# State-space stage: kernel matrix by way of DRAM, per-quarter factors, products summed by accumulating transfers

## The chip, the core and the metric

The kernel runs on one core of a Trainium2 chip. The core has a matrix engine (PE, with its weight loads shown apart as PEld), a vector engine (DVE), a scalar engine (ACT), a general engine (POOL) and a sync engine (SP) whose only work here is to issue transfers. All of them take their instructions in a fixed order and wait on semaphores. Sixteen DMA engines move the data. The metric is device time in microseconds (us). The kernel before takes 2175.32 us, the median of 3 runs (2173.78 to 2179.61).

## The reference

Two layers of a streaming encoder over 256 frames of 2048 channels, in float32. Layer 0 mixes frames with a diagonal state-space model, layer 1 with latent attention; both end in a gated, convolved MLP. The change touches the state-space mixer alone. Its 2048 channels are 128 groups of 16, and each group drives 64 complex states:

```
dt = exp(log_dt);  A = exp(dt * a)                    # per group and state
b' = (A - 1) / a * b
h[t] = A * h[t-1] + b' u[t]                           # u = rmsnorm(x), 16 channels of a group
y[t] = Re(c h[t]) + d_skip * u[t]
y    = gelu(y);  val, gate = split(y @ w_glu + b_glu) # 2048 -> 4096
out  = val * sigmoid(gate)
```

## The kernel before

**Blocks.** The 256 frames are cut into 32 blocks of 8. Within a block, y follows from u by a Toeplitz matrix whose entries are c A^k b' (the kernel matrix), from block to block by the state. The function `s5` goes through the groups in 16 steps (`sb`, 0 to 15) of eight groups (`NG = 2` times `j` 0 to 3); four steps (`PB`) make a quarter of the channels. The 128 partitions hold the real and the imaginary parts of 64 states.

**A step.** `powers` makes, once a quarter, A^0 to A^8 with and without the factor of b' (tile z). `part_a` loads a step's b and c (tile bc, from sBC), scales b with the norm's gain (g4), gives three of the four blocks of bc their signs on ACT (L437 to L439), and multiplies with the powers on DVE: f1 and f2 (output side, nine powers, L448 and L449), e1 and e2 (input side, L451 and L452), and e1 = e1 + e2 (L453). `part_k` turns u (tile U), multiplies f with the last two powers of e on PE to get one row of the kernel matrix (L411, with the skip term L418), copies it to SBUF (tile K, L472), and spreads it to the Toeplitz form: 64 small matmuls with constant selection matrices (C_SL, L482) into two PSUM banks, and two copies to tile TP (L488). `part_e` transposes e1 on PE (L496) and copies it (tile ET, L497). `part_v` multiplies u with ET (tile vs), `part_r` turns vs and rotates it (L515 to L517) and scans over the blocks on DVE (L523), `part_h` rotates back (L528 on PE, L530 to L537 on DVE, tile H), and `part_c` sums TP u and f H on PE and passes the result through Gelu into yg (L549). `frames` makes the sines for the rotations, for two steps at a time (ACT's Sin, L396 and L397).

**The pipeline.** The loop over n issues, in this order: `part_v` of step n-1, `part_c` of n-2, `part_r` of n-1, `part_k` and `part_e` of n, `part_h` of n-1, at the end of a quarter `part_d` (transpose yg and split it into tiles act, L565), then `lead(n+1)`, which is `powers`, `part_a` and `frames` of the next step, and one unit of the matmul with w_glu. So tile TP of a step is read two passes after K was made.

**The w_glu units.** From the first `part_d` on, each pass carries one unit: a load of 1 MB into one of two buffers (raw, L79), a split into a rounded part on ACT (whi, L73) and a rest on DVE (wlo, L74), and 24 matmuls of 512 columns (L108 to L110). 13 of the 32 units lie in the loop; the others follow in `glu_rest`, and then the rest of the network, which the change leaves alone.

**What sets the order.** A list scheduler in the framework orders each engine's instructions when the program is built, with times of its own; the order that it finds is fixed in the program and differs from the written one. All transfers are issued by SP in one queue, in that order: an issue that waits holds up those behind it. Buffers: bc 2, e1 2, e2 1, f1 and f2 3 each, TP 2, raw 2.

Of the kernel before, what the change touches and what calls it, by code (L numbers as in the profile page):

```python
# [40 lines left out]
C_SG, C_NSG, C_TPI, C_FR, C_RS, C_HP, C_MH, C_SL, C_END = 624, 625, 626, 627, 628, 629, 630, 638, 766  # L41
# [3 lines left out]
def tile_trunk(ctx: ExitStack, tc: tile.TileContext, a: dict):  # L45
# [225 lines left out]
    def s5(f):  # L271
        with tc.tile_pool(name="s5", bufs=2) as q1:
# [9 lines left out]
            gX = T(q1, [P, 512], F32, "yg", 1)  # L282
# [50 lines left out]
            Ks = [T(q1, [P, 2, 240], F32, f"K{i}", 1) for i in range(2)]  # L333
            for K in Ks:
                pool.memset(K[:, :, P:], 0.0)
# [5 lines left out]
            dve.tensor_tensor(dB, dB, gX, op=ALU.mult)  # L341
# [14 lines left out]
            def scale_x(rs, qt):  # L356
                c = slice(P * qt, P * qt + P)
                for s in range(8):
                    act.activation(
                        Xn[qt][:, :, 16 * s : 16 * s + 16],  # L360
                        X[s // 4][:, s % 4, c].rearrange("p (g q) -> p g q", q=16),
                        AF.Copy,
                        scale=rs[:, s : s + 1],
                    )

            def powers(qt):
                ps_ = slice(32 * qt, 32 * qt + 32)
# [18 lines left out]
                return z  # L386
# [40 lines left out]
            def flat2(z):  # L427
                return z.rearrange("p s q -> p (s q)")

            def part_a(sb, z):  # L430
# [3 lines left out]
                g4 = T(q1, [P, NP, 16], F32, "g4")  # L434
                sync.dma_start(g4.rearrange("p n q -> p (n q)"), a["sG"][sb].partition_broadcast(P))
                dve.tensor_tensor(bc4[:, 0:2], bc4[:, 0:2], g4.unsqueeze(1).to_broadcast([P, 2, NP, 16]), op=ALU.mult)
                act.activation(bc4[:, 1], bc4[:, 1], AF.Copy, scale=cst[:, C_SG : C_SG + 1])  # L437
                act.activation(bc4[:, 2], bc4[:, 2], AF.Copy, scale=cst[:, C_NSG : C_NSG + 1])
                act.activation(bc4[:, 3], bc4[:, 3], AF.Copy, scale=-1.0)  # L439

                def zt(c, i0, n, t):
                    return z[:, c, i0 : i0 + n, t, h : h + NP].rearrange("p i n -> p n i").unsqueeze(3).to_broadcast([P, NP, n, 16])

                def bc(k, n):
                    return bc4[:, k].unsqueeze(2).to_broadcast([P, NP, n, 16])

                f1, f2 = T(q1, [P, NP, 9, 16], F32, "f1", 3), T(q1, [P, NP, 9, 16], F32, "f2", 3)
                dve.tensor_tensor(f1, zt(0, 0, 9, 1), bc(2, 9), op=ALU.mult)  # L448
                dve.tensor_tensor(f2, zt(1, 0, 9, 1), bc(3, 9), op=ALU.mult)  # L449
                e1, e2 = T(q1, [P, NP, 8, 16], F32, "e1"), T(q1, [P, NP, 8, 16], F32, "e2", 1)  # L450
                dve.tensor_tensor(e1, zt(0, 1, 8, 0), bc(0, 8), op=ALU.mult)  # L451
                dve.tensor_tensor(e2, zt(1, 1, 8, 0), bc(1, 8), op=ALU.mult)  # L452
                dve.tensor_tensor(e1, e1, e2, op=ALU.add)  # L453
                return e1, (f1, f2)

            def part_k(sb, e1, ff):
# [7 lines left out]
                def e67(g, j):  # L464
                    return flat2(e1[:, 4 * g + j, 6:8, :])
# [6 lines left out]
                act.activation(K[:, :, :P], pkg, AF.Copy)  # L472
                TP = T(q1, [P, 4, NG * P], F32, "TP")
                banks = [accb() for _ in range(2)]
                for j in range(2):
                    for odd in range(2):
                        for b in range(4):
                            r = 16 * (2 * b + odd)
                            for jj in range(2):
                                o = C_SL + (2 * j + odd) * 32  # L480
                                hp = slice(64 * jj, 64 * jj + 64)
                                pe.matmul(  # L482
                                    banks[jj][32 * b : 32 * b + 32, j * 256 : (j + 1) * 256].rearrange("p (g c) -> p g c", g=NG),
                                    cst[hp, o : o + 32], K[hp, :, r : r + P],
                                    start=j == 0 and odd == 0, stop=j == 1 and odd == 1, tile_position=(64 * jj, 32 * b),
                                )
                for jj in range(2):
                    act.activation(TP[:, 2 * jj : 2 * jj + 2, :], banks[jj].rearrange("p (j c) -> p j c", j=2), AF.Copy)  # L488
# [51 lines left out]
            def part_c(sb, yg, ff, U, TP, H):  # L540
                def h(g, j):
# [3 lines left out]
                    (lambda g, j: U[:, g, 32 * j : 32 * j + 32], lambda g, j: TP[:, j, g * P : (g + 1) * P]),  # L545
                    *((h, lambda g, j, z=z: flat2(z[:, 4 * g + j, 0:8, :])) for z in ff),
# [5 lines left out]
                    AF.Gelu_apprx_tanh,  # L552
# [40 lines left out]
            for n in range(nb + 2):  # L593
# [522 lines left out]
def _constants():  # L1116
# [8 lines left out]
    c[:, C_DM : C_DM + 16] = (p[:, None] % 32 - 16) == np.arange(16)[None, :]  # L1125
# [11 lines left out]
    for j in range(4):  # L1137
        for odd in range(2):
            q = np.arange(16)
            c[32 * j + 16 + q, C_SL + (2 * (j % 2) + odd) * 32 + 16 * odd + q] = 1.0  # L1140
# [3 lines left out]
def _arrays(i):  # L1144
# [8 lines left out]
    def blocks(re, im):  # L1153
# [18 lines left out]
        "sG": g("norm_g")[0, 0].reshape(4, 16, 2, 16).transpose(1, 2, 0, 3).reshape(16, P),  # L1172
# [37 lines left out]
```

## Time and profile before

| | us |
|---|---|
| median of 3 runs | 2175.32 (2173.78 to 2179.61) |
| the profiled execution | 2179.64, with a span of 2177.9 |
| PE, DVE, ACT, POOL busy in the span | 2080.4, 1402.3, 1130.8, 18.0 |
| state-space loop, from the first product to the last transposes of `part_d` | about 25 to 257 |
| the 16 scans (L523), first and last start | 48.8, 248.7 |
| 64 selection matmuls of all 16 steps (L482) | 33.7 busy on PE |

The times of a row of a view are those of one profiled execution, counted from the first instruction. "busy" adds the durations of the instructions of an engine; two neighbours may overlap by some hundredths of a microsecond, and matmuls by more. "idle before" is time in which the engine stood still ahead of such an instruction, with what ended it. The chain of waits goes back from the last instruction to what released it each time.

### The profile page before, as it was taken

To read this page: it belongs to the slowest core of one execution; us is meant where nothing else is said; L and a number is where in the kernel's file an instruction comes from. 1 tells how busy PE (TensorE), PEld (TensorE's weight loads), DVE (VectorE), ACT (ScalarE), POOL (GpSimd) and SP (SyncE) were. 2 spreads that over 40 slices of the span, in tenths; PEclk is the share of its full clock that TensorE was granted. 3 is DMA by queue.
4 is the path that set the end of the run, shared out by engine and by line. 5 is a ranking of instruction groups with operands and counts; after the bars stand their busy time and mean duration, and the time that the engine had idled before them with its cause. 6 is when DMAs were issued, how large, how long until landed. Compare 5 with 4: busy or idle time off the path is not lost.

```text
span 2177.9 us, 32720 instructions
## 1 busy us (share of the span) xinstructions
PE 2080.4 (96%) x13396; PEld 1769.9 (81%) x13396; DVE 1402.3 (64%) x1956; ACT 1130.8 (52%) x1743; POOL 18.0 (1%) x57
## 2 busy tenths in 40 slices
PE   3789989999999999999999999999999999999997
PEld 2566767888888888888878998888888888888886
DVE  8999665666466556655676665566646655665567
ACT  6677444655455435544464554555445544553444
POOL 0000000000000000000000000000000000000000
PEclk9999999999999999999999999999999999999999
DMA  4132466455565565556564434646555656555654
GB/s 132 45 103 76 137 209 207 147 186 183 193 194 193 174 202 185 193 180 204 183 201 141 136 117 154 215 133 194 177 193 194 194 175 202 186 192 184 202 187 144
DMA packets 280967, 372.68 MB, mean 171 GB/s; under 512 B 9456, under 2 KB 196464, under 8 KB 280048
## 3 DMA queue, kind: packets, MB, share of 16 engines
q1 hardware_dynamic: 280816, 370.58, 52.2%
q8 instruction: 105, 1.72, 0.3%
q14 instruction: 46, 0.38, 0.1%
HBM read 368.46 MB, written 2.10 MB: 170 GB/s over the span
## 4 chain that ended last, share of the span: by engine, by line
PE 80%; DVE 8%; DMA 6%; ACT 4%; issue 1%; POOL 0%; SPq 0%; DVEq 0%; POOLq 0%; ACTq 0%
PE wk L727 28%; PE wk L729 14%; PE acc L110 9%; PE acc L109 9%; PE acc L108 9%; DMA raw<-in_w_glu 3%; PE wk L109 2%; PE wk L110 2%; PE wk L108 2%; DVE wlo L74 2%; ACT whi L73 1%; DVE x L74 1%; DMA raw<-in_w_o 1%; ACT junk L135 1%; PE acc L189 1%
## 5 line engine op out<-in xcount | busy, mean ns | idle before, releaser
L74 DVE TENSOR_TENSOR wlo<-raw,whi 128x1024 fp32r<-128x1024 f32 (+1 forms) x636 | 755.6, 1191 | 613.7 <-ACT whi L73 610.3
L73 ACT ACTIVATE whi<-raw 128x1024 fp32r<-128x1024 f32 (+1 forms) x636 | 653.9, 1031 | 756.9 <-PE wk L727 322.5
L727 PE MATMUL wk<-act,whi 128*128 128x512 f32 x2688 | 673.5, 392 | 0.0
L727 PEld LDWEIGHTS wk<-act,whi 128*128 128x128 f32 x2688 | 483.8, 189 | 86.8
L729 PEld LDWEIGHTS wk<-act,wlo 128*128 128x128 f32 x2688 | 366.7, 190 | 26.2
L729 PE MATMUL wk<-act,wlo 128*128 128x256 f32 x2688 | 374.8, 282 | 0.0
L109 PE MATMUL acc<-wlo,hh 128*128 128x512 f32 x652 | 255.7, 392 | 0.0
L110 PE MATMUL acc<-whi,hl 128*128 128x512 f32 x652 | 255.7, 394 | 0.0
L108 PE MATMUL acc<-whi,hh 128*128 128x512 f32 x652 | 253.4, 389 | 0.0
L109 PEld LDWEIGHTS acc<-wlo,hh 128*128 128x128 f32 x652 | 122.4, 188 | 28.0
L108 PEld LDWEIGHTS acc<-whi,hh 128*128 128x128 f32 x652 | 122.4, 188 | 27.5 <-ACT hh L73 0.5
L110 PEld LDWEIGHTS acc<-whi,hl 128*128 128x128 f32 x652 | 122.6, 188 | 24.7
L108 PE MATMUL acc<-whi,act 128*128 128x512 f32 (+1 forms) x316 | 120.8, 383 | 1.7 <-ACT whi L73 1.4
L109 PE MATMUL acc<-wlo,act 128*128 128x512 f32 (+1 forms) x316 | 119.1, 377 | 2.6 <-DVE wlo L74 2.6
L110 PE MATMUL acc<-whi,act 128*128 128x512 f32 (+1 forms) x316 | 118.3, 375 | 0.0
L786 DVE SCALAR_TENSOR_TENSOR cv<-gs,cw,cv 128x255 f32<-128x255 f32 (+1 forms) x168 | 80.9, 482 | 17.2 <-ACT cv L784 14.2
L784 ACT ACTIVATE cv<-gs,cb,cw 128x256 f32<-128x256 f32 x84 | 49.9, 594 | 45.8 <-DVE gs L735 45.8
L109 PEld LDWEIGHTS acc<-wlo,act 128*128 128x128 f32 x316 | 59.8, 189 | 14.9 <-DVE wlo L74 4.6
L108 PEld LDWEIGHTS acc<-whi,act 128*128 128x128 f32 x316 | 59.8, 189 | 13.4 <-ACT whi L73 2.2
L110 PEld LDWEIGHTS acc<-whi,act 128*128 128x128 f32 x316 | 59.7, 189 | 10.8 <-issue 0.4
L74 DVE TENSOR_TENSOR x<-raw,x 128x1024 fp32r<-128x1024 f32 x36 | 43.2, 1221 | 28.4 <-ACT x L73 28.3
L108 PE MATMUL acc<-x,act 128*128 128x512 f32 (+1 forms) x164 | 56.6, 347 | 4.1 <-DVE act L197 3.6
(282 smaller groups left out, 2336.5 us busy)
## 6 DMA issues: line engine op xcount, KB each, us to landing
raw<-in_w_gate SPq DMA_DIRECT2D x88, 1024.0 KB, 5.1
raw<-in_w_up SPq DMA_DIRECT2D x88, 1024.0 KB, 5.1
raw<-in_w_down SPq DMA_DIRECT2D x88, 1024.0 KB, 5.0
raw<-in_w_glu SPq DMA_DIRECT2D x32, 1024.0 KB, 6.0
raw<-in_w_o SPq DMA_DIRECT2D x16, 1024.0 KB, 5.0
raw<-in_w_ukv SPq DMA_DIRECT2D x8, 1024.0 KB, 5.4
raw<-in_w_uq SPq DMA_DIRECT2D x8, 768.0 KB, 4.6
bc<-in_sBC SPq DMA_DIRECT2D x16, 256.0 KB, 2.7
```

The source lines that it names most:

```text
L73: act.activation(hi, src, AF.Copy)
L74: (eng or dve).tensor_tensor(lo, src, hi.bitcast(F32), op=ALU.subtract)
L108: pe.matmul(o, lh, rh, start=first, stop=False)
L109: pe.matmul(o, lh, rl, start=False, stop=False)
L110: pe.matmul(o, ll, rh, start=False, stop=last)
L135: act.activation(junk[:, :w], src, AF.Square, accum_out=stat)
L189: pe.matmul(ptv[:, k, :], h[:, o : o + P], d, start=True, stop=True)
L727: pe.matmul(o, w, pair(kt), start=kt == 0, stop=False)
L729: pe.matmul(o[:, 0, :], w, pair(kt)[:, 0], start=False, stop=kt == KT - 1)
L784: act.activation(cv[:, ft, :], gv[:, ft, :], AF.Identity, scale=cw[:, 2, n : n + 1], bias=cb[:, n : n + 1])
L786: dve.scalar_tensor_tensor(cv[:, ft, sh:], gv[:, ft, : S - sh], cw[:, 2 - sh, n : n + 1], cv[:, ft, sh:], op0=ALU.mult, op1=ALU.add,)
```

## The change

**Kernel matrix.** The powers are cut to eight on the output side, and the row of the kernel matrix comes from f and b itself (a slice of tile bc) in place of f and the last two powers of e, so `part_k` no longer reads e1. Tile K is laid out with the two groups interleaved. It is written to a DRAM tile kd (L477, 128 rows of 480 floats), and TP is read back from there by four transfers, each of 128 rows of 256 floats that overlap in DRAM (L481). The selection matrices, the 64 matmuls and the two copies of a step are gone.

**Factors per quarter.** The signs go into four copies of the powers (tile zs, L390 to L393, ACT, once a quarter) in place of three scalings of bc in each step. The norm's gain is multiplied into x (L358, DVE, two instructions of 128 x 512 in each quarter) in place of b (g4 and its loads are gone) and d_skip. Gelu is applied to all of yg once a quarter, in `part_d` (L558); each step copies its part into yg (L545).

**The sum.** e1 + e2 is done by a transfer that POOL issues: it reads e2 and adds it into e1, both 128 x 1024 floats in SBUF (L454).

```diff
+                zs = T(q1, [P, 4, 8, 32], F32, "zs")
+                act.activation(zs[:, 1], z[:, 1, 0:8, 1, :], AF.Copy, scale=cst[:, C_SG : C_SG + 1])
+                act.activation(zs[:, 2], z[:, 0, 1:9, 0, :], AF.Copy, scale=cst[:, C_NSG : C_NSG + 1])
+                act.activation(zs[:, 3], z[:, 1, 1:9, 0, :], AF.Copy, scale=-1.0)
+                act.activation(zs[:, 0], z[:, 0, 0:8, 1, :], AF.Copy)
...
             def scale_x(rs, qt):
                 c = slice(P * qt, P * qt + P)
+                for h in range(2):
+                    dve.tensor_tensor(
+                        X[h][:, :, c], X[h][:, :, c], gX[:, c].unsqueeze(1).to_broadcast([P, 4, P]), op=ALU.mult
+                    )
...
-                sync.dma_start(g4.rearrange("p n q -> p (n q)"), a["sG"][sb].partition_broadcast(P))
-                dve.tensor_tensor(bc4[:, 0:2], bc4[:, 0:2], g4.unsqueeze(1).to_broadcast([P, 2, NP, 16]), op=ALU.mult)
-                act.activation(bc4[:, 1], bc4[:, 1], AF.Copy, scale=cst[:, C_SG : C_SG + 1])
-                act.activation(bc4[:, 2], bc4[:, 2], AF.Copy, scale=cst[:, C_NSG : C_NSG + 1])
-                act.activation(bc4[:, 3], bc4[:, 3], AF.Copy, scale=-1.0)
...
-                dve.tensor_tensor(f1, zt(0, 0, 9, 1), bc(2, 9), op=ALU.mult)
-                dve.tensor_tensor(f2, zt(1, 0, 9, 1), bc(3, 9), op=ALU.mult)
-                dve.tensor_tensor(e1, zt(0, 1, 8, 0), bc(0, 8), op=ALU.mult)
-                dve.tensor_tensor(e2, zt(1, 1, 8, 0), bc(1, 8), op=ALU.mult)
-                dve.tensor_tensor(e1, e1, e2, op=ALU.add)
+                dve.tensor_tensor(f1, zt(2), bc(2), op=ALU.mult)
+                dve.tensor_tensor(f2, zt(3), bc(3), op=ALU.mult)
+                dve.tensor_tensor(e1, zt(0), bc(0), op=ALU.mult)
+                dve.tensor_tensor(e2, zt(1), bc(1), op=ALU.mult)
+                pool.dma_start(e1, e2, accum_op=ALU.add)
...
-                act.activation(K[:, :, :P], pkg, AF.Copy)
-                banks = [accb() for _ in range(2)]
...
-                for jj in range(2):
-                    act.activation(TP[:, 2 * jj : 2 * jj + 2, :], banks[jj].rearrange("p (j c) -> p j c", j=2), AF.Copy)
+                act.activation(K[:, : NG * P].rearrange("p (c g) -> p g c", g=NG), pkg, AF.Copy)
+                kd = T(dr, [P, 240 * NG], F32, "kd", 3)
+                sync.dma_start(kd, K)
+                TP = T(q1, [P, 4, P * NG], F32, "TP")
+                for j in range(4):
+                    rows = kd[32 * j : 32 * j + 16, :]
+                    sync.dma_start(
+                        TP[:, j, :],
+                        bass.AP(rows.tensor, rows.offset, [[16 * NG, 8], [240 * NG, 16], [1, P * NG]]),
+                    )
...
-                    AF.Gelu_apprx_tanh,
+                    AF.Copy,
...
             def part_d(qt, yg):
                 act_tiles()
+                act.activation(yg, yg, AF.Gelu_apprx_tanh)
```

Since the scheduler orders the program, the edits also move instructions that the diff does not show. Three places follow; the numbers behind a name are those of the buffers' tiles, so equal numbers are the same data.

On DVE, the products of the first three steps. Before (e1_71, e1_88 and e1_112 are e1 of steps 0, 1 and 2, L453 the additions):

```order
L448 TENSOR_TENSOR f1_69_243<-z_60_212,bc_67_235 128x1152
L449 TENSOR_TENSOR f2_70_244<-z_60_212,bc_67_235 128x1152
L451 TENSOR_TENSOR e1_71_247<-z_60_212,bc_67_235 128x1024
L452 TENSOR_TENSOR e2_72_248<-z_60_212,bc_67_235 128x1024
L448 TENSOR_TENSOR f1_86_353<-z_60_212,bc_84_345 128x1152
L453 TENSOR_TENSOR e1_71_247<-e1_71_247,e2_72_248 128x1024
L449 TENSOR_TENSOR f2_87_354<-z_60_212,bc_84_345 128x1152
L451 TENSOR_TENSOR e1_88_357<-z_60_212,bc_84_345 128x1024
L452 TENSOR_TENSOR e2_89_358<-z_60_212,bc_84_345 128x1024
L436 TENSOR_TENSOR bc_108_479<-bc_108_479,g4_109_481 128x256
L453 TENSOR_TENSOR e1_88_357<-e1_88_357,e2_89_358 128x1024
L448 TENSOR_TENSOR f1_110_487<-z_60_212,bc_108_479 128x1152
```

And now, from the instruction behind e2 of step 0 on (e1_84 and e1_106 are e1 of steps 1 and 2; L453 is now the second product, which the transfer adds):

```order
L450 TENSOR_TENSOR f1_86_321<-zs_67_236,bc_83_317 128x1024
L451 TENSOR_TENSOR f2_87_322<-zs_67_236,bc_83_317 128x1024
L452 TENSOR_TENSOR e1_84_319<-zs_67_236,bc_83_317 128x1024
L450 TENSOR_TENSOR f1_108_421<-zs_67_236,bc_105_417 128x1024
L453 TENSOR_TENSOR e2_85_320<-zs_67_236,bc_83_317 128x1024
L451 TENSOR_TENSOR f2_109_422<-zs_67_236,bc_105_417 128x1024
L452 TENSOR_TENSOR e1_106_419<-zs_67_236,bc_105_417 128x1024
L511 TENSOR_TENSOR w1_91_355<-wk_90_350,co_74_253 128x256
L512 TENSOR_TENSOR w2_92_356<-wk_90_350,si_73_252 128x256
L358 TENSOR_TENSOR raw_14_96<-raw_14_96,gX_16_106 128x4x128
L513 TENSOR_TENSOR w1_91_355<-w1_91_355,w2_92_356 128x256
L453 TENSOR_TENSOR e2_107_420<-zs_67_236,bc_105_417 128x1024
```

The additions are gone, and four instructions stand ahead of the e2 of step 1, six more ahead of that of step 2, among them the rotation of step 0 (w1_91 and w2_92) and a multiplication of x (raw_14).

On SP, the stretch with the second load of w_glu. Before:

```order
L433 DMA bc_108_479<-in_sBC 128x512
L79 DMA raw_231_1187<-in_w_glu 128x4x512
L79 DMA raw_264_1378<-in_w_glu 128x4x512
L433 DMA bc_136_648<-in_sBC 128x512
L435 DMA g4_169_833<-in_sG 128x128
L433 DMA bc_168_831<-in_sBC 128x512
L435 DMA g4_196_993<-in_sG 128x128
L435 DMA g4_224_1164<-in_sG 128x128
L79 DMA raw_305_1599<-in_w_glu 128x4x512
L433 DMA bc_195_991<-in_sBC 128x512
L433 DMA bc_223_1162<-in_sBC 128x512
```

And now (kd_97 and kd_123 are the writes of K of steps 1 and 2, TP_98 and TP_124 the reads, the bc rows the loads of later steps):

```order
L477 DMA kd_97_390<-K1_46_185 128x480
L79 DMA raw_220_985<-in_w_glu 128x4x512
L481 DMA TP_98_392<-kd_97_390 128x1x256 x4
L477 DMA kd_123_525<-K0_45_184 128x480
L441 DMA bc_162_706<-in_sBC 128x512
L79 DMA raw_251_1140<-in_w_glu 128x4x512
L481 DMA TP_124_527<-kd_123_525 128x1x256 x4
L441 DMA bc_187_830<-in_sBC 128x512
L477 DMA kd_146_651<-K1_46_185 128x480
L481 DMA TP_147_653<-kd_146_651 128x1x256 x4
```

The loads of g4 are gone; each step has a write and four reads, and the loads raw_220 and raw_251 of w_glu stand between a write and its reads.

On PE, step 5 from the rows of the kernel matrix to the rotation. Before (wk_210 the row of the kernel matrix, e1_199 this step's e1):

```order
L411 MATMUL wk_210_1064<-f2_198_1000,e1_199_1003 32x128 x4
L411 MATMUL wk_210_1064<-f1_197_999,e1_199_1003 32x128 x4
L411 MATMUL wk_210_1064<-f2_198_1000,e1_199_1003 32x128 x4
L418 MATMUL wk_210_1064<-dB_17_105,cst_1_73 32x2x16 x4
L496 MATMUL wk_215_1124<-cst_1_73,e1_199_1003 128x128 x4
L482 MATMUL acc_212_1087<-K1_46_183,cst_1_73 32x256
L482 MATMUL acc_213_1088<-K1_46_183,cst_1_73 32x256
L482 MATMUL acc_212_1087<-K1_46_183,cst_1_73 32x256
L482 MATMUL acc_213_1088<-K1_46_183,cst_1_73 32x256
```

And now (wk_201 is that row, wk_194 the sums of `part_c` of step 3, e1_188 this step's e1):

```order
L419 MATMUL wk_194_853<-f2_135_557,H1_50_191 32x128 x4
L419 MATMUL wk_194_853<-TP_147_653,U_144_627 32x128 x4
L419 MATMUL wk_194_853<-f1_134_556,H1_50_191 32x128 x4
L419 MATMUL wk_194_853<-f2_135_557,H1_50_191 32x128 x4
L419 MATMUL wk_201_897<-f2_191_835,bc_187_830 32x128 x3
L426 MATMUL wk_201_897<-dB_17_107,cst_1_73 32x2x16 x4
L492 MATMUL wk_205_927<-cst_1_73,e1_188_832 128x128 x4
L492 MATMUL wk_206_933<-cst_1_73,e1_188_832 128x128 x4
L524 MATMUL wk_207_939<-R_198_890,cst_1_73 128x256
L562 MATMUL wk_211_948<-cst_1_73,yg_114_458 128x128 x4
```

The 64 selection matmuls that stood amid or behind the transposes of e1 are gone, the transposes follow the skip term, and behind them stand the rotation of the step before (L524) and the transposes of yg (L562).

More of the change, by code (lines that the diff above doesn't have):

```diff
@@ L40 @@
 C_ID, C_PS, C_PR, C_BO, C_DM, C_MK, C_CV = 0, 128, 256, 384, 512, 528, 592
-C_SG, C_NSG, C_TPI, C_FR, C_RS, C_HP, C_MH, C_SL, C_END = 624, 625, 626, 627, 628, 629, 630, 638, 766
+C_SG, C_NSG, C_TPI, C_FR, C_RS, C_HP, C_MH, C_END = 624, 625, 626, 627, 628, 629, 630, 638
 @with_exitstack
@@ L271, in s5 @@
     def s5(f):
-        with tc.tile_pool(name="s5", bufs=2) as q1:
+        with tc.tile_pool(name="s5", bufs=2) as q1, tc.tile_pool(name="dr", bufs=2, space=bass.MemoryType.DRAM) as dr:
             w0 = env["wp"]
@@ L281, in s5 @@
                 sync.dma_start(X[k // 4][:, k % 4, :], a["xs"][k])
-            gX = T(q1, [P, 512], F32, "yg", 1)
+            gX = T(q1, [P, 512], F32, "gX", 1)
             dB = T(q1, [P, 512], F32, "dB", 1)
@@ L332, in s5 @@
             dve.tensor_tensor(th, th, tn, op=ALU.subtract)
-            Ks = [T(q1, [P, 2, 240], F32, f"K{i}", 1) for i in range(2)]
+            Ks = [T(q1, [P, 240 * 2], F32, f"K{i}", 1) for i in range(2)]
             for K in Ks:
-                pool.memset(K[:, :, P:], 0.0)
+                pool.memset(K[:, 2 * P :], 0.0)
             Ds = [T(q1, [P, 8, 32], F32, f"dc{i}", 1) for i in range(2)]
@@ L340, in s5 @@
             dmask = cst[:, C_DM : C_DM + 16]
-            dve.tensor_tensor(dB, dB, gX, op=ALU.mult)
             dve.tensor_tensor(
@@ L385, in powers @@
                     dve.tensor_tensor(v(o)[:, 1], u[:, 1], w[:, 0], op=ALU.add)
-                return z
+                zs = T(q1, [P, 4, 8, 32], F32, "zs")
[3 more added lines that the diff above has]
+                act.activation(zs[:, 0], z[:, 0, 0:8, 1, :], AF.Copy)
+                return zs
             def frames(k):
@@ L433, in part_a, with zt, bc, part_k @@
                 sync.dma_start(bc4, a["sBC"][sb])
[L434 to L438, printed above, removed]
-                act.activation(bc4[:, 3], bc4[:, 3], AF.Copy, scale=-1.0)
[L441 to L450, printed above, removed]
-                dve.tensor_tensor(e1, zt(0, 1, 8, 0), bc(0, 8), op=ALU.mult)
[L452 to L456, printed above, removed]
+                def zt(i):
+                    return z[:, i, :, h : h + NP].rearrange("p i n -> p n i").unsqueeze(3).to_broadcast([P, NP, 8, 16])
+                def bc(k):
+                    return bc4[:, k].unsqueeze(2).to_broadcast([P, NP, 8, 16])
+                e1, e2, f1, f2 = (T(q1, [P, NP, 8, 16], F32, t, b) for t, b in (("e1", 2), ("e2", 1), ("f1", 3), ("f2", 3)))
+                dve.tensor_tensor(f1, zt(2), bc(2), op=ALU.mult)
[3 more added lines that the diff above has]
+                pool.dma_start(e1, e2, accum_op=ALU.add)
+                return e1, (f1, f2), bc4
+            def part_k(sb, ff, bc4):
                 puv = wk()[:, : NG * P].rearrange("p (g t) -> p g t", g=NG)
@@ L462, in part_k, with b1 @@
                 act.activation(U, puv, AF.Copy)
-                def e67(g, j):
-                    return flat2(e1[:, 4 * g + j, 6:8, :])
+                bw = bc4.rearrange("p k n q -> p (k n q)")
+                def b1(g, j):
+                    return bw[:, 16 * (4 * g + j) : 16 * (4 * g + j) + 32]
                 skip = dB.rearrange("p (g q) -> p g q", q=16)[:, NG * sb : NG * (sb + 1), :]
                 pkg = by_group(
-                    tiled(*((e67, lambda g, j, z=z: flat2(z[:, 4 * g + j, 1:9, :])) for z in ff), diag=skip)
+                    tiled(*((b1, lambda g, j, z=z: flat2(z[:, 4 * g + j])) for z in ff), diag=skip)
                 )
                 K = Ks[sb % 2]
-                act.activation(K[:, :, :P], pkg, AF.Copy)
-                TP = T(q1, [P, 4, NG * P], F32, "TP")
-                banks = [accb() for _ in range(2)]
[L475 to L478, printed above, removed]
-                            for jj in range(2):
[L480 to L488, printed above, removed]
+                act.activation(K[:, : NG * P].rearrange("p (c g) -> p g c", g=NG), pkg, AF.Copy)
[8 more added lines that the diff above has]
+                    )
                 return U, TP
@@ L544, in part_c @@
                 py = tiled(
-                    (lambda g, j: U[:, g, 32 * j : 32 * j + 32], lambda g, j: TP[:, j, g * P : (g + 1) * P]),
-                    *((h, lambda g, j, z=z: flat2(z[:, 4 * g + j, 0:8, :])) for z in ff),
+                    (lambda g, j: U[:, g, 32 * j : 32 * j + 32], lambda g, j: TP[:, j, :].rearrange("p (c g) -> p g c", g=NG)[:, g, :]),
+                    *((h, lambda g, j, z=z: flat2(z[:, 4 * g + j])) for z in ff),
                 )
@@ L603, in s5 @@
                 if n < nb:
-                    U[n], TP[n] = part_k(n, *ab[n])
+                    U[n], TP[n] = part_k(n, *ab[n][1:])
                     ET[n] = part_e(ab[n][0])
@@ L1124, in _constants @@
     c[:, C_BO : C_BO + P] = (p[:, None] % 32) == (p[None, :] % 32)
-    c[:, C_DM : C_DM + 16] = (p[:, None] % 32 - 16) == np.arange(16)[None, :]
+    c[:, C_DM : C_DM + 16] = (p[:, None] % 32) == np.arange(16)[None, :]
     c[:64, C_MK : C_MK + 64] = -1e30
@@ L1136, in _constants @@
     c[:, C_MH : C_MH + 8] = -0.5
[L1137 to L1140, printed above, removed]
     return c
@@ L1171, in _arrays @@
         ),
-        "sG": g("norm_g")[0, 0].reshape(4, 16, 2, 16).transpose(1, 2, 0, 3).reshape(16, P),
         "gX": np.repeat(g("norm_g")[0, 0].reshape(4, 512), 32, 0),
```

## The prediction

> **What bounds the kernel now.** I read the page first, then busy time by stretch, then the chain of waits, and last the groups and transfers of the state-space loop. The page says where the time is:
>
> ```profile
> PE 2080.4 (96%) x13396; PEld 1769.9 (81%) x13396; DVE 1402.3 (64%) x1956; ACT 1130.8 (52%) x1743; POOL 18.0 (1%) x57
> PE   3789989999999999999999999999999999999997
> DVE  8999665666466556655676665566646655665567
> ```
>
> PE is full nearly everywhere, but in the first four or five slices (54 us each) it is not, and there DVE is. That is the loop which the change edits. By stretch (PE, PEld, DVE, ACT, POOL, granted clock, DMA share, GB/s):
>
> ```profile
> 20.00:98.00 78.00, 49.45 (x994) 35.22 (x994) 73.55 (x119) 49.40 (x122) 0.64 (x3) 0.93 0.25 73
> 98.00:160.00 62.00, 55.11 (x838) 42.11 (x839) 57.32 (x89) 46.84 (x90) 0.25 (x4) 0.97 0.32 90
> 160.00:218.00 58.00, 51.10 (x822) 38.95 (x820) 53.80 (x77) 44.12 (x81) 0.00 (x0) 0.94 0.25 72
> 218.00:256.00 38.00, 36.98 (x564) 28.74 (x563) 24.96 (x41) 18.69 (x34) 0.00 (x0) 1.00 0.20 58
> 256.00:400.00 144.00, 132.78 (x592) 104.76 (x591) 95.08 (x133) 72.79 (x104) 1.60 (x4) 1.00 0.68 213
> ```
>
> From 20 to 98 (steps 0 to 4, no w_glu unit on PE yet) DVE is busy 94% and PE 63%. From 98 to 218 both are near 90%, DVE 92% and 93%, PE 89% and 88%; from 218 PE alone binds (97%). DMA has room. The chain of waits agrees: it runs along DVE, with PE's selection matmuls and ACT's table loads between (start, us, what):
>
> ```profile
> 56.43 1.13 DVE e L453
> 57.90 1.27 DVE f L448
> 59.77 1.26 DVE f L449
> 74.05 0.60 DVE si L392
> 74.65 0.34 DVE bc L436
> 170.04 1.89 PE acc L482 x64
> 182.42 1.28 ACT L549
> ```
>
> These are what an instruction adds to the chain, a little less than its duration, because neighbours overlap; I use them as prices. A microsecond less for DVE in the loop ends the loop a microsecond sooner, as long as PE loses as much from 98 on. What follows the loop keeps its instruction order, so an earlier end is passed on.
>
> **The change part by part.** Of DVE's groups (busy, mean ns, idle before):
>
> ```profile
> L448 DVE TENSOR_TENSOR f<-z,bc 128x1152 f32<-128x1152 f32 x16 | 21.6, 1351 | 1.0 <-PE wk L411 1.0
> L452 DVE TENSOR_TENSOR e<-z,bc 128x1024 f32<-128x1024 f32 x16 | 19.5, 1218 | 0.9 <-ACT bc L437 0.9
> L453 DVE TENSOR_TENSOR e<-e,e 128x1024 f32<-128x1024 f32 x16 | 19.4, 1214 | 0.0
> L436 DVE TENSOR_TENSOR bc<-bc,g 128x256 f32<-128x256 f32 x16 | 6.7, 418 | 3.8 <-DMA bc<-in_sBC 3.6
> L392 DVE TENSOR_TENSOR si<-th,cst 128x512 f32<-128x512 f32 x8 | 5.4, 683 | 0.0
> ```
>
> Each of 16 steps loses the addition (1.13), the gain on b (0.34), and an eighth of f1 and f2, which come down from 1152 to the 1024 elements of e (1.27 to 1.13, twice: 0.28). That is 1.75 a step, 28.0 us in all. The gain on d_skip goes once (0.60). Added are eight instructions of 128 x 512 on x, 0.60 each by L392: 4.8. Net on DVE: 28.0 + 0.6 - 4.8 = 23.8.
>
> On PE and ACT:
>
> ```profile
> L482 PE MATMUL acc<-K,cst 64*32 64x256 f32 x1024 | 33.7, 401 | 0.0
> L488 ACT ACTIVATE TP<-acc 128x512 f32<-128x512 f32 x32 | 17.1, 586 | 2.3 <-PE acc L482 2.3
> L549 ACT ACT_TABLE_LOAD x11 | 14.1, 1283 | 2.3 <-PE wk L411 2.1
> L396 ACT ACT_TABLE_LOAD x6 | 7.7, 1283 | 0.1
> L438 ACT ACTIVATE bc<-bc,cst 128x128 f32<-128x128 f32 x16 | 6.4, 400 | 8.0 <-DMA bc<-in_sBC 7.9
> L503 ACT ACTIVATE vs<-wk 128x256 f32<-128x256 f32 x16 | 6.1, 384 | 1.5 <-PE wk L411 1.5
> L73 ACT ACTIVATE whi<-raw 128x1024 fp32r<-128x1024 f32 x56 | 58.9, 1056 | 69.4 <-DMA raw<-in_w_glu 36.2 <-PE acc L110 24.4 <-PE wk L110 8.9
> ```
>
> PE loses the selection matmuls, 1.89 a step by the chain. In the eleven steps from 98 on that is 20.8, against DVE's 11 x 1.75 = 19.3. So neither engine keeps the old length, and DVE's sum decides. ACT loses per step two copies of TP (0.59 each), three scalings like L438 (0.40) and most table loads, and gains per quarter four sign copies like L503 (0.38) and a Gelu over 128 x 1024 (1.06 by L73). It was busy 49.40 of 78 and 44.12 of 58, so its relief is worth nothing by itself; what hides it is DVE's work. Some loads lie on the chain (1.28 at 182.42), so relief there could give up to some 4 us; I take none of it and keep it for the range. The four sign copies stand between the powers and the first products: four times 0.38, some 1.5 us once, later quarters being made ahead. The net is 23.8 - 1.5 = 22.3.
>
> **The new wait.** e1 is now complete only when POOL's transfer has landed, and e2, which has one buffer, cannot be written again before. No transfer like it is in the trace. The nearest, with size and median us from issue to landing:
>
> ```profile
> bc<-in_sBC SPq DMA_DIRECT2D x16, 256.0 KB, 2.7
> raw<-in_w_dkv SPq DMA_DIRECT2D x1, 512.0 KB, 4.3
> raw<-in_w_down SPq DMA_DIRECT2D x88, 1024.0 KB, 5.0
> raw<-in_w_glu SPq DMA_DIRECT2D x32, 1024.0 KB, 6.0
> out<-x SPq DMA_DIRECT2D x8, 256.0 KB, 2.5
> ```
>
> A plain 512 KB lies between 2.7 and 5.0, about 3.5 on that line; that is the lower bound. The addition also reads its destination, which makes it as heavy as 1 MB, 5.0 to 6.0; if POOL needs time to start it and the write counts as a third pass, up to 9. I take 6.0, the row of 1 MB beside other traffic. Who waits? In the new DVE order, the work between one e2 and the next, at the prices above, is 4.5 us (four products of 1.13, steps 0 and 1), 3.9 (two products, three small ones at 0.34, one at 0.60), 4.0, later 5.4, 3.6 and 3.9; elsewhere it is over 7. With 6.0 DVE waits 1.5 + 2.1 + 2.0 + 0.6 + 2.4 + 2.1 = 10.7 us. On PE the transposes of e1 wait, and behind them the rotation (L524), which DVE's H needs; from e2 to there stand five to seven microseconds of DVE's and PE's other work, so I put the point from which each of ten steps loses too at 6.5. One old wait disappears in the new ones:
>
> ```profile
> 46.48 0.42 DVE L515 TENSOR_TENSOR w<-wk,co 128x256 f32<-128x256 f32 x1 [2.83 <-PE wk L513]
> ```
>
> There DVE stood 2.8 us for step 0's first rotation; now it waits for e2 instead while PE catches up. Sum: 22.3 - 10.7 + 2.8 = 14.4 us.
>
> [...]
>
> **The way through DRAM.** K is written (2.5 by out, also a write of 256 KB), then read by four transfers of 128 KB, together 512 KB (3.5 to 6, four issues), about 10 us from K to TP with its issues. The gap that it has to fit in is from K's copy to the sum that needs TP:
>
> ```profile
> 34.52 0.39 ACT L472 ACTIVATE K<-wk 128x256 f32<-128x256 f32 x1 [1.15 <-PE wk L418]
> 57.27 0.38 ACT L549 ACTIVATE yg<-wk 128x256 f32<-128x256 f32 x1 [0.42 <-PE wk L411]
> ```
>
> 22 us for step 0, two passes for every step. Two passes of other work hide it, and I cost it at nothing; without them it would be 10 us a step. But SP issues in order, and it waits for buffers of w_glu:
>
> ```profile
> SPq L79 <- DVE wlo L74: 165.5, 26, 20.8
> L435 SPq DMA_DIRECT2D g<-in_sG x16: 327/328/383, 12.5 to 173.3; - x16
> ```
>
> 26 waits of 165.5 us in the first 400 (longest 20.8): the reads behind such a load are held as long. Issues themselves take 0.33 us: five more a step and one fewer (g4), 1.3 us a step on a queue that mostly waits. Loads of bc now wait for PE's reading of bc in `part_k`, a few microseconds later than f2; they had 1.1 to 1.3 us too little before (L436's 3.6 in all), and no longer feed a DVE instruction of their own.
>
> **The rivals.**
>
> *The adding transfer is too slow.* This ends on the other side. At 9 us, DVE waits 28.7 at the six places and ten steps lose 2.5 each: 22.3 + 2.8 - 28.7 - 25 = -28.6, so slower by 29, 2204. The point from which it decides: at 7.1 the six places take 17.3 and ten steps 6, and the gain is near 2. For it: 6.0 is my own choice between ends far apart, and traffic goes up by about 1.3 MB a step over 14 us, some 90 GB/s on 72 to 90. Against it: a DMA share of 0.25 to 0.32, and most e2 are far apart. POOL's start is the special risk: if POOL is held up by a DVE that is busy 94%, the transfer starts late by an instruction or two of 1.13 us, which alone makes 6.0 into 8. [...]
>
> *The transfer is quick.* At 4 us or below nothing waits but 0.5 us; with the table loads it gives 22.3 + 4 = 26, and 2149.
>
> *TP comes late through SP.* Loads of w_glu stand between a write of K and its reads in six places of the new order. Were each held 5 us longer than two passes cover, 30 us would go, and 14.4 - 30 leaves 16 slower, 2191. For it: the 20.8 above. Against it: the gap of 22 is twice the path, and the loads held are those that DVE frees before.
>
> *No passing on.* After the loop the chain goes over loads of w_glu (DMA share 0.68 from 256 to 400). If these set their own pace from the start, the gain stays in the loop and the time is 2175. Against: a load starts when a buffer comes free, which moves with the loop.
>
> **How the numbers follow.** The profiled execution took 2179.64 (span 2177.9), 4.3 above the median of 2175.32. 14.4 less is 2165.2 on its terms and 2160.9 on the median's; I say 2161. Chances: the forecast (transfer between 4.5 and 6.8 us) 0.46, its own range 2153 to 2170; quick transfer 0.13; too slow 0.25; SP 0.08; no passing on 0.08. Differences under 0.3% (6.5 us) cannot be told from no change. Nearly all of the first two cases is faster, less a part of the first near 6.6 us: 0.56. Slower, from the third and fourth less what lies near the turning point: 0.30. The same: 0.14. The range for 8 in 10 leaves out the quickest cases and the longer part of the slow ones: 2148 to 2192.
>
> **What would show it.** Right: POOL's transfers land in 5 to 7 us; the first and the last scan (48.8 and 248.7 before) lie some 15 us nearer; DVE's idle time is led by e2 waiting for that transfer, six times by 1 to 3 us; nothing waits for TP; the stretch after the loop is as long as before. Wrong: a landing over 7 us with e2 or e1's transposes waiting in every step; PE waiting for TP; or the loop shorter and the w_glu units behind it longer by as much.

## The result, and the profile after

The changed kernel takes 2162.14 us, the median of 6 runs (2154.14 to 2165.59), against 2176.62 for the kernel before (6 runs, 2173.78 to 2181.74). The ratio is 0.9931, with a 95% interval of 0.9914 to 0.9948: 14.5 us less. The profiled execution took 2165.37, with a span of 2163.6, 14.3 less than before.

Both kernels issue the same instructions in the same order behind the state-space stage. So the first matmul of the layer's MLP is a mark that both pass (view of one line; the two times at its end are the first and the last start):

```profile
L727 PE MATMUL wk<-act,whi x2688: 389/389/481, 425.8 to 2142.7; 128*128 128x512 f32 x192
```

```profile
L724 PE MATMUL wk<-act,whi x2688: 389/389/477, 411.9 to 2129.9; 128*128 128x512 f32 x192
```

The mark moves by 13.9, so nearly all of the gain is made ahead of it, and what follows passes it on. Busy time up to the mark, before and after (PE, PEld, DVE, ACT, POOL, granted clock, DMA share, GB/s):

```profile
0.00:425.80 425.80, 350.27 (x4007) 274.08 (x4008) 332.71 (x530) 258.08 (x492) 7.12 (x32) 0.98 0.43 130
```

```profile
0.00:411.90 411.90, 329.46 (x2983) 262.78 (x2984) 307.85 (x505) 219.05 (x418) 21.21 (x48) 0.95 0.65 182
```

| up to the mark, us | before | after | difference |
|---|---|---|---|
| DVE busy | 332.7 | 307.9 | -24.9 |
| DVE idle | 93.1 | 104.1 | +11.0 |
| PE busy | 350.3 | 329.5 | -20.8 |
| PE idle | 75.5 | 82.4 | +6.9 |

DVE does 25 us less and waits 11 more. PE has lost 33.7 us of selection matmuls, but is only 20.8 less busy: the 2983 matmuls that are left take longer together, at a granted clock of 0.95 in place of 0.98. The stretches of the loop, as they were shown of before:

```profile
20.00:98.00 78.00, 42.03 (x626) 31.55 (x626) 63.49 (x107) 37.09 (x97) 6.61 (x11) 0.85 0.62 159
98.00:160.00 62.00, 55.12 (x700) 43.48 (x699) 56.17 (x89) 41.69 (x78) 3.47 (x4) 0.97 0.71 190
160.00:218.00 58.00, 49.57 (x590) 38.94 (x592) 47.64 (x78) 31.11 (x58) 3.47 (x4) 0.91 0.66 168
218.00:256.00 38.00, 35.71 (x346) 28.50 (x335) 26.72 (x41) 15.87 (x25) 1.01 (x3) 0.96 0.64 181
256.00:400.00 144.00, 134.62 (x640) 108.23 (x638) 96.67 (x145) 74.93 (x116) 3.24 (x7) 0.99 0.70 212
```

In the first stretch DVE is busy 81% where it was 94%. The fifth scan starts at 93.4, where it started at 93.2: the first five steps gain nothing. The last scan starts at 236.4 in place of 248.7. The gain lies in the steps from the sixth on, where ten take 126.0 us in place of 135.7.

Waits from 20 to 250 (engine and what waits, what for, total, times, longest), of DVE and then of PE:

```profile
DVE w L511 <- PE wk L509: 10.1, 6, 5.9
DVE f L268 <- PE acc L110: 9.9, 4, 3.7
DVE e L453 <- DMA e<-e: 7.5, 4, 3.3
DVE w L527 <- PE wk L524: 3.6, 3, 2.1
```

```profile
PE wk L492 <- DMA e<-e: 20.8, 5, 8.2
PE wk L524 <- DVE R L519: 4.8, 6, 2.2
PE wk L419 <- DMA TP<-kd: 2.4, 1, 2.4
```

DVE waits for the transfer (e2, L453) 7.5 us, less than for PE's turned products (L511, 10.1 in place of 5.7 before) and for PE's sums of the w_glu units (L268, 9.9 in place of 1.9). PE waits for it (e1's transposes, L492) 20.8 us, the longest 8.2. Not all of this is new: 6.7 of it stands in the first step, where PE stood 7.7 for DVE's addition in the kernel before:

```profile
PE wk L411 <- DVE e L453: 7.7, 1, 7.7
```

The transfer itself, with POOL's time for the issue in ns and its landing:

```profile
L454 POOL DMA_DIRECT2D e<-e x16: 859/865/1052, 32.4 to 220.5; - x16
DMA to landing us min/median/max: 4.6/5.9/8.4
```

### The profile page after: what moved, and what is told of

It is laid out like the page before. It is cut to its first block, busy times and chain, and to the rows that moved or that the text cites. A ratio compares the mean times of both kernels' runs of the same rounds, so it can differ in the third digit from the quotient of the medians.

```text
span 2163.6 us, 30716 instructions
## 1 busy us (share of the span) xinstructions
PE 2059.6 (95%) x12372; PEld 1758.9 (81%) x12372; DVE 1378.3 (64%) x1931; ACT 1091.9 (50%) x1669; POOL 32.2 (1%) x73
## 4 chain that ended last, share of the span: by engine, by line
PE 81%; DMA 4%; DVE 3%; ACT 2%; issue 1%; POOL 0%; POOLq 0%; DVEq 0%; ACTq 0%; SPq 0%
PE wk L724 28%; PE wk L726 15%; PE acc L109 9%; PE acc L110 9%; PE acc L108 9%; PE wk L109 2%; PE wk L110 2%; PE wk L108 2%; DMA raw<-in_w_glu 2%; DVE wlo L74 1%; DVE x L74 1%; ACT whi L73 1%; PE acc L189 1%; DMA raw<-in_w_o 1%; DMA e<-e 1%
## 5 line engine op out<-in xcount | busy, mean ns | idle before, releaser
L783 DVE SCALAR_TENSOR_TENSOR cv<-gs,cw,cv 128x255 f32<-128x255 f32 (+1 forms) x168 | 81.0, 482 | 17.2 <-ACT cv L781 14.3
L110 PEld LDWEIGHTS acc<-whi,act 128*128 128x128 f32 x316 | 60.8, 192 | 10.7 <-issue 0.2
```

Source lines behind the costliest of these rows:

```text
L110: pe.matmul(o, ll, rh, start=False, stop=last)
L783: dve.scalar_tensor_tensor(cv[:, ft, sh:], gv[:, ft, : S - sh], cw[:, 2 - sh, n : n + 1], cv[:, ft, sh:], op0=ALU.mult, op1=ALU.add,)
```

## The experiments

Each is compared with the kernel before on the same chip, and its difference from the changed kernel is that of the two ratios. Only the plain copy keeps the order of the instructions; in all the others the scheduler makes a new one, so that a difference holds the edit and the new order together.

| run | median us | ratio to before, 95% | fifth scan | last scan | ten steps |
|---|---|---|---|---|---|
| before | 2176.62 | 1 | 93.2 | 248.7 | 135.7 |
| changed | 2162.14 | 0.9931 (0.9914 to 0.9948) | 93.4 | 236.4 | 126.0 |
| plain copy | 2150.62 | 0.9878 (0.9860 to 0.9896) | 87.4 | 220.3 | 116.0 |
| no sum | 2143.74 | 0.9845 (0.9832 to 0.9859) | 78.2 | 215.6 | 123.8 |
| transfer twice | 2208.25 | 1.0139 (1.0123 to 1.0154) | 110.0 | 274.4 | 142.2 |
| factors only | 2170.43 | 0.9971 (0.9962 to 0.9981) | 86.0 | 245.4 | 138.1 |
| factors and DRAM | 2173.07 | 0.9981 (0.9969 to 0.9992) | 88.5 | 240.7 | 136.7 |
| factors and transfer | 2183.66 | 1.0042 (1.0029 to 1.0055) | 100.9 | 255.6 | 135.1 |
| before, with transfer | 2200.85 | 1.0114 (1.0098 to 1.0129) | 106.9 | 271.4 | 145.7 |
| two buffers for e2 | 2163.28 | 0.9941 (0.9926 to 0.9955) | 90.4 | 233.1 | 126.3 |
| added on DVE in steps 0 to 4 | 2172.79 | 0.9972 (0.9961 to 0.9983) | 85.5 | 239.3 | 135.9 |
| added on DVE in steps 0 and 4 | 2174.77 | 0.9991 (0.9980 to 1.0002) | 89.4 | 243.5 | 133.3 |
| DRAM by ACT's queue | 2170.35 | 0.9971 (0.9960 to 0.9982) | 93.0 | 237.5 | 126.2 |
| e ahead of f, two buffers | 2168.21 | 0.9970 (0.9958 to 0.9981) | 86.6 | 234.7 | 131.5 |

The scans' starts are of the profiled executions; "ten steps" is from the sixth scan to the last.

### Which part pays

One part undone, two undone, and one alone.

```diff
-                pool.dma_start(e1, e2, accum_op=ALU.add)
+                dve.tensor_tensor(e1, e1, e2, op=ALU.add)
```

> The changed kernel, with e1 + e2 added on DVE again and no accumulating transfer. Theory of the prediction (DVE sets the loop's end): 16 additions of 1.13 come back, 18.1 us, and DVE's waits for e2, 7.5 us in the trace after, go: some 10.6 us slower than the changed kernel, about 2173. Rival (the transfer costs as much as it saves, since PE too waits for it, 20.8 us in the trace after): within 4 us of the changed kernel, 2158 to 2166.

```diff
-                kd = T(dr, [P, 240 * NG], F32, "kd", 3)
-                sync.dma_start(kd, K)
...
+                banks = [accb() for _ in range(2)]
+                for j in range(2):
...
+                                pe.matmul(
...
+                for jj in range(2):
+                    act.activation(TP[:, 2 * jj : 2 * jj + 2, :], banks[jj].rearrange("p (j c) -> p j c", j=2), AF.Copy)
```

> The changed kernel, with the kernel matrix spread by the 64 selection matmuls and two copies again in place of the way through DRAM; all else as changed. Theory (the way through DRAM is hidden but for PE's one wait of 5.3 us for TP, and takes 1.9 us a step from a PE that is near full from the sixth step on): 11 x 1.9 = 21 us slower less 5: about 2178. Rival (DVE alone sets the end, PE's relief gives nothing, and the traffic through DRAM holds other transfers up): as fast or faster than the changed kernel, 2152 to 2163.

Both of these edits together:

> The changed kernel with both undone, so that of the change only the eight powers, the signs, the gain and Gelu per quarter are left. Theory: DVE is spared (0.34 + 0.28) x 16 + 0.6 = 10.5 and gets 4.8 and 1.5 us, PE nothing: 4 us faster than the kernel before, 2172. Rival (ACT's table loads and scalings, 14 loads and 48 scalings fewer, lie on the path): 8 us or more faster, 2168 or less.

And the transfer in the kernel before, alone:

```diff
-                dve.tensor_tensor(e1, e1, e2, op=ALU.add)
+                pool.dma_start(e1, e2, accum_op=ALU.add)
```

> The kernel before, with e1 + e2 by the accumulating transfer and nothing else changed. Theory: DVE is spared 18.1 us and waits some 8 for e2: 10 us faster, 2166; with less other traffic the transfer lands in about 5 us in place of 5.9. Rival (from the sixth step on PE with its selection matmuls sets the end, so that only the first five steps gain): 2 to 5 us faster, or no faster at all.

Measured: 2173.07, 2183.66, 2170.43 and 2200.85. The first is the number of DVE's sum, 18.1 of additions less 7.5 of waits, but by luck: against the run without any sum, shown further down, the transfer costs 18.7 in place of 7.5, and the additions on DVE cost 29.6 in place of 18.1 (each in an order of its own). The second goes the way of its theory, 5.7 us further. The factors alone give 6.3, where the sum without the additions gives 22.3 - 18.1 = 4.2 and the rival 8 or more; the interval (4.1 to 8.3) does not decide between the two.

The way through DRAM, added to them, gives nothing (2170.43 to 2173.07): PE is spared 1.9 us a step, and the ten steps are only 1.4 us shorter. The transfer, added to the factors, costs 13.2 us, and added to the kernel before it costs 24. Together with the way through DRAM it gains: 2173.07 to 2162.14. So the parts do not add up, and of the transfer alone both theory and rival fell: it loses. Where it is lost, in the kernel before with the transfer (DVE, then PE, 20 to 257):

```profile
DVE e L452 <- DMA e<-e: 27.2, 11, 7.1
```

```profile
PE wk L411 <- DMA e<-e: 16.0, 1, 16.0
```

There the order has the next e2 so close behind the transfer that DVE waits in 11 of 16 steps, though the transfer lands in 4.9 at the median. These losses may lie in the orders that the scheduler made and not in PE's load; no run holds the order and takes the way through DRAM away. With the factors and the transfer, the fifth scan is 14.9 late against the factors alone (100.9 and 86.0), and later steps win back little: DVE is then waiting for its data elsewhere.

```profile
DVE wlo L74 <- ACT whi L73: 16.2, 8, 4.1
DVE e L453 <- DMA bc<-in_sBC: 9.8, 6, 3.7
DVE e L453 <- DMA e<-e: 6.7, 2, 4.0
```

### What the time to the landing is worth, with the order held

The transfer copies e2 over e1 in place of adding (so the sum is left out); the order is the same on every engine.

```diff
-                pool.dma_start(e1, e2, accum_op=ALU.add)
+                pool.dma_start(e1, e2)
```

> The changed kernel with POOL's transfer as a plain copy of e2 over e1 in place of the addition, so that the output is that of e2 alone; the order of the instructions is the same on every engine. It shows what the adding costs against a plain 512 KB, and what the time until the landing is worth with the order held. Theory of the prediction (a plain 512 KB lands in about 3.5, the addition makes it as heavy as 1 MB, 5.9; each us matters where DVE and PE wait): landing 3.5 to 4, DVE's waits for e2 gone, 6 to 10 us faster than the changed kernel, 2152 to 2156. Rival (the landing is set by POOL's start and the traffic, not by the adding): landing above 5, time as the changed kernel's, 2160 to 2164.

Measured: 2150.62. The line of the transfer, and PE's and DVE's waits for it:

```profile
L454 POOL DMA_DIRECT2D e<-e x16: 527/528/711, 32.1 to 205.7; - x16
DMA to landing us min/median/max: 2.9/4.0/7.1
```

```profile
PE wk L492 <- DMA e<-e: 6.6, 2, 5.9
```

```profile
DVE e L453 <- DMA e<-e: 2.0, 2, 1.7
```

Landing falls from 5.9 to 4.0, PE's wait from 20.8 to 6.6, DVE's from 7.5 to 2.0, and the time by 11.5, where 6 to 10 were expected: some 6 us for each us of landing. The copy moves the same bytes, but its packets hold the DMA engines half as long (POOL's queue from 20 to 250: packets, MB, share of 16 engines; the changed kernel, then the copy):

```profile
q0 software_dynamic: 2304, 8.39, 21.1%
```

```profile
q0 software_dynamic: 2304, 8.39, 10.2%
```

What that does to the other transfers is in the 11.5 too; this run does not part it from the landing. DVE is as busy as in the changed kernel up to the mark, 307.7 of 398.9; its idle time, 91.2, is that of before (93.1). So at a landing of 4.0 DVE no longer pays for the change in idle time.

Leaving the transfer out altogether, and doubling it (the second waits for the first, so e1 is complete after 5.6 + 6.0); here the order is a new one:

```diff
-                pool.dma_start(e1, e2, accum_op=ALU.add)
```

> The changed kernel without the addition: neither DVE nor a transfer adds e2 to e1, the output is that of e1 alone. It shows what all waits for the transfer are worth. Theory (7.5 us of DVE's idle time and a PE that waits for e1 in the first steps): 8 to 12 us faster than the changed kernel, 2150 to 2154. Rival (the waits of the trace only take the place of others): at most 4 us faster, 2158 or more.

```diff
                 pool.dma_start(e1, e2, accum_op=ALU.add)
+                pool.dma_start(e1, e2, accum_op=ALU.add)
```

> The changed kernel with the accumulating transfer issued twice, one behind the other, so that e2 is added twice and e1 is complete after some 11.8 us in place of 5.9. By the prediction's price (six places of DVE work 3.6 to 5.4 us apart lose the rest, ten steps lose what exceeds 6.5): 45 + 53 us lost against 25 saved, about 2250. Rival (in most steps later work covers it, and only the first five steps lose some 6 us each): about 2192.

Measured: 2143.74 and 2208.25. All waits together are worth 18.7, with the new order, more than expected; the fifth scan alone starts 15 us earlier (78.2 and 93.4). The doubled one costs 45, half of what the price of the prediction gives and more than the rival's 30, though DVE does wait in 13 steps and PE in 9:

```profile
DVE e L453 <- DMA e<-e: 36.2, 13, 7.9
```

```profile
PE wk L493 <- DMA e<-e: 49.2, 9, 13.1
```

### Where the wait sits

Two buffers for e2, so that DVE need not wait:

```diff
-                e1, e2, f1, f2 = (T(q1, [P, NP, 8, 16], F32, t, b) for t, b in (("e1", 2), ("e2", 1), ("f1", 3), ("f2", 3)))
+                e1, e2, f1, f2 = (T(q1, [P, NP, 8, 16], F32, t, b) for t, b in (("e1", 2), ("e2p", 2), ("f1", 3), ("f2", 3)))
```

> The changed kernel with two buffers for e2, so that DVE need not wait for the transfer before it writes the next e2. Theory (DVE's waits for e2, 7.5 us, are lost on the engine that sets the end): 4 to 8 us faster than the changed kernel, 2154 to 2158. Rival (PE waits for e1 all the same, and DVE then waits for PE): 2160 to 2164.

Measured: 2163.28, no difference. DVE's wait for e2 is gone, and PE's is just as long:

```profile
PE wk L492 <- DMA e<-e2p: 20.8, 4, 7.8
```

```profile
DVE w L527 <- PE wk L524: 11.2, 9, 3.5
DVE w L511 <- PE wk L509: 10.8, 6, 7.4
```

DVE no longer waits for the transfer, and waits 7.6 more for PE in its place (L527: 11.2 in place of 3.6). This points to e1's transposes as the wait that costs; it does not show it, since the order is new (DVE's waits at L268 fell from 9.9 to 4.4, for one). The next two put the addition back on DVE where PE waited, in the first steps:

```diff
-                pool.dma_start(e1, e2, accum_op=ALU.add)
+                if sb < 5:
+                    dve.tensor_tensor(e1, e1, e2, op=ALU.add)
+                else:
+                    pool.dma_start(e1, e2, accum_op=ALU.add)
```

> The changed kernel, with e1 + e2 on DVE in steps 0 to 4 and by the accumulating transfer from step 5 on. Theory (the transfer costs in the first five steps, where nothing covers it, and pays later): the fifth scan starts at about 88.5, as with all additions on DVE, in place of 93.4, and from there a step takes 11.4 us as in the changed kernel: 5 us faster than that, about 2157. Rival (what the first steps lose comes back from slack later, or the additions there cost 5 x 1.13 = 5.6 as much as the waits): 2162, no difference.

> The changed kernel, with the addition on DVE in steps 0 and 4 alone, the two whose e1 PE waited longest for (6.7 and 8.2 us). Theory (those two waits are what the transfer costs in the beginning): 2 to 8 us faster than the changed kernel, 2154 to 2160. Rival (DVE waits for e2 set the beginning, and these two additions only add 2.3 us): 2162 to 2165.

(The second has `sb in (0, 4)`.) Measured: 2172.79 and 2174.77, both slower than the changed kernel; both theories and both rivals fell. In the first of them the fifth scan does start earlier, even at 85.5. But the ten steps then take 135.9 in place of 126.0, though all have the transfer. The order was made anew, and in it PE waits for e1 12.6 us in steps where it waited 5.9 (1.5, 2.4 and 1.9) in the changed kernel. What the engine stood still for ahead of these transposes:

```profile
  DMA e<-e: 12.6, 4
  DVE e L455: 8.2, 3
```

The 6.7 us more at the transfer stand against 9.9 us of longer steps; the rest stays open. The last run wrote e1, e2 and the transfer ahead of f1 and f2, with two buffers for e2:

```diff
-                dve.tensor_tensor(f1, zt(2), bc(2), op=ALU.mult)
-                dve.tensor_tensor(f2, zt(3), bc(3), op=ALU.mult)
                 dve.tensor_tensor(e1, zt(0), bc(0), op=ALU.mult)
                 dve.tensor_tensor(e2, zt(1), bc(1), op=ALU.mult)
                 pool.dma_start(e1, e2, accum_op=ALU.add)
+                dve.tensor_tensor(f1, zt(2), bc(2), op=ALU.mult)
+                dve.tensor_tensor(f2, zt(3), bc(3), op=ALU.mult)
```

> The changed kernel with two buffers for e2 and with e1, e2 and the transfer written ahead of f1 and f2, so that in the first steps e2 stands one or two products (1.13 us each) earlier in DVE's order; the comparison is with two buffers alone (2163). Theory (what costs is the time until e1 has landed, some 6 us in all for each us by the plain copy): 5 to 10 us faster, 2153 to 2158. Rival (PE's rows of the kernel matrix need f and stand ahead of e1's transposes in PE's order, so that f is waited for in place of e1): 2161 or more.

Measured: 2168.21, slower than two buffers alone. The fifth scan starts at 86.6 in place of 90.4, and PE's wait for e1 falls from 20.8 to 4.5, so much of the theory held. But the rival's wait is there (PE for f, 4.0 us in three places), and the ten steps take 131.5 in place of 126.3.

### TP through another queue

The write of K and the four reads issued by ACT:

```diff
-                sync.dma_start(kd, K)
+                act.dma_start(kd, K)
...
-                    sync.dma_start(
+                    act.dma_start(
                         TP[:, j, :],
```

> The changed kernel with the write of K and the reads of TP issued by ACT in place of SP, so that they stand behind no load of w_glu and no load of w_glu behind them. Theory (the one late TP, 5.3 us of PE and 5.9 of DVE, came from that queue): 3 to 6 us faster than the changed kernel, 2156 to 2159. Rival (it was late because the transfers share the DMA engines with 1 MB loads, and ACT loses five issues a step): 2162 or more.

Measured: 2170.35, 9 slower. TP is late once here too: the reads for step 1 go out from 48.3, and PE waits 4.3 us for them until 62.85. So it was not SP's queue alone that made them late; whether the traffic on the DMA engines did stays open. And the time that ACT spends on issues is waited for (0.60 us at the median for one read of TP; ACT's copy L499 stands behind these reads for 22.3 us in six places):

```profile
PE wk L508 <- ACT vs L499: 17.1, 10, 4.5
```

In the changed kernel that wait is 2.2.

## Why the prediction was right, and where it was not

The forecast was 2161, and 14.4 us of gain; measured are 2162.1 and 14.5. Step by step:

**DVE's work.** Forecast 23.8 less; measured 24.9 less up to the mark. Right. The products now:

```profile
L450 DVE TENSOR_TENSOR f<-zs,bc 128x1024 f32<-128x1024 f32 x16 | 19.5, 1217 | 2.2 <-PE wk L419 1.9 <-ACT zs L391 0.2
L453 DVE TENSOR_TENSOR e<-zs,bc 128x1024 f32<-128x1024 f32 x16 | 19.5, 1221 | 7.6 <-DMA e<-e 7.5
```

Waits for the sign copies are 0.2, not 1.5: the products of the norm's gain stand in that gap on DVE, and the first product starts at 27.4 in place of 25.1.

**The landing.** Taken at 6.0, measured 5.9. The lower bound was too low: a plain copy of the same size takes 4.0, not 3.5. The reason given for 6.0, that the addition is as heavy as twice the bytes, holds in the packets' time: 21.1% and 10.2% of the DMA engines. The special risk did not come: POOL's issue starts 0.3 to 0.7 us behind the end of the later product and takes 0.86 to 1.05, beside a DVE that is busy 81% to 91% from 20 to 218.

**Who waits.** This is the step that failed, though its sum came out. It put 10.7 us of waits at DVE's e2, and put the point from which PE's transposes matter at 6.5. Measured: at a landing of 5.9 DVE waits 7.5, in four places and not six, and PE waits 20.8, some 14 of it where it did not wait for the sum before. Three rows of DVE's first steps:

```profile
38.22 1.23 DVE L453 TENSOR_TENSOR e<-zs,bc 128x1024 f32<-128x1024 f32 x1 [1.40 <-DMA e<-e]
44.95 1.22 DVE L453 TENSOR_TENSOR e<-zs,bc 128x1024 f32<-128x1024 f32 x1
52.40 1.23 DVE L453 TENSOR_TENSOR e<-zs,bc 128x1024 f32<-128x1024 f32 x1 [1.34 <-DMA e<-e]
```

The first was forecast at 1.5, the third at 2.0; the second, at 2.1, is not there, since DVE had just waited 1.6 for PE. And with two buffers DVE's wait goes and the time stays. In the sum 10.7 - 2.8 + 1.5 = 9.4 of idle time stands against 11.0 measured. That the two are close is luck: the terms are others. Of what the prediction charged at e2, 3.2 us did not come; waits for PE's turned products went from 5.7 to 10.1 (the old stall of 2.8, taken as won back, is still 1.6), and those for PE's sums of the w_glu units from 1.9 to 9.9. That DVE pays by way of PE for the same landing fits the plain copy, where with PE's wait for e1 (20.8 to 6.6) these two fall as well, to 7.7 and 4.9; the longest of them, 5.9, has another cause, told below.

**Neither engine alone.** That DVE's sum decides fits one run: PE's relief, added to the factors, does not move the time. That the transfer loses 13 and 24 us where the selection matmuls are still there was not foreseen; whether it needs PE's relief or met a worse order is not shown.

**The way through DRAM.** Costed at nothing. It is late once, for step 1. K's write was issued at 46.0, the reads from 48.9 on (0.58 us for one issue at the median, where 0.33 was put), and PE waits for them until 62.9: the path took 17 us in place of about 10, and PE came to its sum 14.4 us behind that write, where the prediction reckoned with a gap of 22 for step 0:

```profile
  PEld wk L419: 2.9, 1
  PE wk L419: 2.4, 1
```

The two rows are one stretch of time, that of the weight load and that of the matmul behind it, so PE loses 2.4 and not their sum of 5.3, with which the expectations reckon. Behind it DVE stands 5.9 us, the longest of its waits. The traffic came out as forecast, 86 to 100 GB/s more from 20 to 218. Of the 30 us that the rival put on late TP, this one wait came.

**The rivals' prices.** "Quick" at 4 us was given as 2149, 12 us below the forecast for 2 us of landing; the copy that lands in 4.0 takes 2150.6, 11.5 less for 1.9. The size is right, but 4 of those 12 were table loads that no run prices. "Too slow" was priced at 43 us for the step from 6 to 9, 14 per us; the doubled transfer, at 11.6, costs 45, 8 per us. The prediction added the waits at e2 and at e1. In the doubled run they are 36.2 and 49.2 us, together nearly twice what the doubling costs, so they are not to be added. The gain was passed on: 2.7 at the first scan, where some 15 had been given as a sign, 12.3 at the last and 13.9 at the mark.

## What to carry to other kernels

An addition moved from a full engine to a transfer pays less by the waits for the landing (here some 6 us for each us of landing, with the order held): ask on every engine who reads the result first, not only who must write its buffer again. Parts of a change need not add up (here the transfer lost 13 to 24 us in two kernels and gained 10.9 in a third), so test them together as well as alone. And where a scheduler makes the order, a small edit can move as much time as the one under test; an edit that keeps the order (here the plain copy) is what gives a price.

## What had not been expected of the hardware

A short wait of PE cost more here than itself. In the chain of waits of the changed kernel, PE waits 2.4 us for e1's last but one transfer (start, us, what; each row with acc is one matmul of 512 columns):

```profile
202.40 5.96 DMA e<-e
208.36 0.14 issue
208.49 0.52 PE wk L492 x3
209.01 0.23 PE acc L109
...
210.08 0.43 PE acc L110
210.50 0.43 PE acc L108
...
212.64 0.43 PE acc L108
213.06 0.29 PE acc L109
213.36 0.25 PE acc L110
```

From 1.2 us behind it on, for 3.4 us, a matmul takes up to 0.43 in place of 0.23: nine of them lose 1.6 us. The granted clock (the number before the last two) falls by half for that time, and again behind the wait of 1.9 that ends at 225.75:

```profile
206.24:209.65 3.41, 1.16 (x7) 1.05 (x8) 3.41 (x6) 2.96 (x5) 0.00 (x0) 1.00 0.73 187
209.65:213.06 3.41, 3.41 (x10) 2.64 (x9) 0.24 (x1) 0.62 (x2) 0.00 (x0) 0.50 0.96 307
226.70:230.10 3.40, 3.40 (x11) 2.67 (x10) 1.13 (x3) 0.85 (x2) 0.00 (x0) 0.50 0.89 247
```

It does not follow every such wait: behind the one of 1.5 that ends at 181.00, the clock stays at 1.00 (180.20 to 185.77). With the additions on DVE in steps 0 to 4, PE waits for the transfer three times between 100 and 240 (7.2 us in all, the longest 2.7), its last transposes of e1 are released at 230.2, and from 218 to 256 the clock is 1.00. In the run with the plain copy PE does not wait at the place of the 1.9 (the transposes start at 209.95), and the matmuls behind it keep 0.23; up to the mark PE is there 324.6 busy in place of 329.5, at a clock of 0.97 in place of 0.95. So the same 2983 matmuls take 4.9 us longer in the changed kernel; how much of that is in the 13.0 us between these two profiles at the mark is not shown.
